# A decoder trunk on eight cores: sums of squares on VectorE, a list scheduler for the order, weights loaded once per tile

**The chip, the cores and the metric.** One Trainium2 chip, all eight cores, two dies of four cores (0 to 3 and 4 to 7). The metric is the device time of the slowest core in microseconds. Executions come in a fast state and a slow one: in the slow state the cores of one die (or of both) show a lower granted TensorE clock and the time is longer. Below, fast runs are compared with fast runs; where a kernel left no fast run, the cores of an undisturbed die are compared, and the text says so.

## The reference, cut to what matters

Four layers on x of (4, 8192, 1024). Even layers mix tokens with a gMLP (spatial gating inside chunks of 128 tokens), odd ones with causal pooling; a SwiGLU of width 2816 follows each. Every sub-layer has an RMS norm in front and one behind.

```python
def rmsnorm(x, g):
    y = xf * lax.rsqrt(jnp.mean(xf * xf, axis=-1, keepdims=True) + EPS)
    ...
def mixer_a(h, ...):
    z = gelu(h @ w_in);  u, v = split(z);  v = layernorm(v)
    sv = einsum('gts,bnsgd->bntgd', tril(w_s), v) + b_s      # 128x128 per group
    return (u * sv) @ w_out
def swiglu(h, ...):
    return (silu(h @ w_gate) * (h @ w_up)) @ w_down
for i in range(4):
    x = x + rmsnorm(mixer(rmsnorm(x, pre)), post)            # A if i even, B if odd
    x = x + rmsnorm(swiglu(rmsnorm(x, pre2)), post2)
```

Each core has half a sequence: 4096 tokens and some earlier ones (the halo) that the mixers look back to.

## The kernel before

Features lie on partitions (8 chunks of 128), tokens on the free axis. A core goes through five tiles of 896 tokens, each split in a half of 512 and one of 384 columns. So that TensorE has work while the norms between two sub-layers run, the output projection goes half by half, and the chain of norms of the first half is meant to lie behind the projection of the second.

An RMS norm needs a sum over partitions. ScalarE squares each of the eight chunks, and a matmul with a matrix of ones adds each square into a PSUM bank, which then holds the sum on every partition:

```python
def stats_mm(fc, first, last):
    pe_mm(PSH(sb_), ONESM[:], SQv(fc), first, last, ...)     # one matmul per square

# PostNorm.chain: steps of a boundary, each with a time worked out by hand
d = (n + 60) / 960.0
a = (n + 240) / 1200.0
r1 = 1.0 + 1.3 + 2 * a + 0.5
for fc in range(1, KC):
    th.append(lambda fc=fc: mult(fc));     times.append(r1 + i * d); i += 1
    th.append(lambda fc=fc: add(fc - 1));  times.append(r1 + i * d); i += 1
    th.append(pre[fc - 1])                 # square + stats_mm of the next norm
    ...
def tick(dt):                              # called after each group of matmuls
    clock["t"] += dt
    while bg and bg[0][0] <= clock["t"]:
        bg.pop(0)[1]()                     # emit the steps that are due by that clock
```

So the program order of every engine is what these estimated times make of it. Weights go through three slots of 1 MB of bf16 (the DMA casts them from fp32: the page of before has 1321 MB read from HBM, where the weight queue moved 650 MB). The code is written to load output weights once for each half, unless a slot still has them; the profile counts 260 loads for SwiGLU's where one for each tile would be 160, 40 for pooling's instead of 20, and only 50 instead of 40 for mixer A's:

```python
NWSLOT = 3
def run_sublayer(hA, hB, head, mid, tail, make_chain, reuse=False):
    ...
    for p, first, last in natural_order(tail):
        p.load(); p.run(hA, first, last)
    drain_all(); add_chain(make_chain(hA))
    for p, first, last in (reuse_order(tail) if reuse else natural_order(tail)):
        p.load(); p.run(hB, first, last)   # load() does nothing if the slot still has it
    drain_all(); add_chain(make_chain(hB))
```

The spatial gating of mixer A comes in one go after all u projections: for each of 16 chunks of 128 features a few matmuls of 128 columns fill a bank, VectorE adds a bias out of that bank and multiplies by u.

Of the kernel before, what the change touches and what calls it, by code (L numbers as in the profile page):

```python
# [14 lines left out]
NCH = 7  # L15
T = NCH * 128
HALVES = ((0, 512), (512, 384))
NTILES = 5
HALO = 3
NCHUNK = NTILES * NCH  # L20
NTOK = NCHUNK * 128
OWN = 4096
DFF = 2816
NJ = DFF // 128
EPS = 1e-6
WSLOT = 4096
NWSLOT = 3
USE_LNEXP = True

GC_MIXPRE, GC_MIXPOST, GC_FFNPRE, GC_FFNPOST, GC_BSCALE, GC_LNB, GC_N = 0, 32, 64, 96, 128, 144, 176  # L30

class Op:
    __slots__ = ("eng", "fn", "deps", "sig", "sigidx", "dsem", "dval", "pos", "gidx", "clk", "ckey")

    def __init__(self, eng, fn, dsem=None, dval=0):
        self.eng = eng
        self.fn = fn
        self.deps = []
        self.sig = False
        self.sigidx = 0  # L40
        self.dsem = dsem
        self.dval = dval

class Sched:
# [9 lines left out]
    def add(self, eng, fn, reads=(), writes=(), dsem=None):  # L54
# [13 lines left out]
        for k in reads:  # L68
            rec = res.get(k)
            if rec is not None and rec[0] is not None:  # L70
                deps[id(rec[0])] = (rec[0], "RAW")
        for k in writes:
            rec = res.get(k)
            if rec is not None:
                if rec[0] is not None and id(rec[0]) not in deps:
                    deps[id(rec[0])] = (rec[0], "WAW")
                for r in rec[1]:
                    if id(r) not in deps:
                        deps[id(r)] = (r, "WAR")
        cand = []  # L80
        for d, kind in deps.values():
            if d is op:
                continue
            if d.dsem is None and op.dsem is None and d.eng == eng:
                if eng == "pe":
                    continue
            cand.append(d)
# [10 lines left out]
        if op.dsem is None:  # L98
            clk[op.ckey] = op.pos
        else:  # L100
            clk[op.ckey] = op.pos
# [71 lines left out]
def build_nc(layers=(0, 1, 2, 3), ntiles=NTILES):  # L173
    nc = bass.Bass("TRN2", target_bir_lowering=False)
    S = Sched()
# [6 lines left out]
    a_w_in = dram("a_w_in", [2, D, 4096])  # L182
    a_w_out = dram("a_w_out", [2, 2048, D])
    b_w_in = dram("b_w_in", [2, D, D])
    b_w_grp = dram("b_w_grp", [2, 4, 256, 256])
    b_w_out = dram("b_w_out", [2, D, D])
    w_gate = dram("ffn_w_gate", [4, D, DFF])
    w_up = dram("ffn_w_up", [4, D, DFF])
    w_down = dram("ffn_w_down", [4, DFF, D])
    gvec_d = dram("gvec", [128, GC_N])  # L190
    lng_d = dram("a_ln_g", [2, 2048])
# [3 lines left out]
    pm_d = dram("poolm", [3, 128, 512])  # L195

    sb = nc.alloc_sbuf_tensor
    X = sb("X", [128, KC * T], F32)
    H = sb("H", [128, KC * T], BF16)
    MS = sb("MS", [128, KC * T], F32)  # L200
    SQ = sb("SQ", [128, KC * T], BF16)
    BIG = sb("BIG", [128, 28672], BF16)
    WR = sb("WR", [128, NWSLOT * WSLOT], BF16)
    RS = [sb("RS0", [128, T], F32)]
    SG = [sb("SG0", [128, T], BF16)]
    GV = sb("GV", [128, GC_N], F32)
    GBC = sb("GBC", [128, 2 * 2048], BF16)
    WSM = sb("WSM", [128, 2 * 1024], BF16)
    BIAS = sb("BIAS", [128, 2 * 2048], F32)
    PM = sb("PM", [128, 3 * 512], BF16)  # L210
    PH = sb("PH", [128, 2 * 1024], BF16)
    ONESM = sb("ONESM", [128, 128], BF16)
    ONES1 = sb("ONES1", [128, 128], BF16)
    EPSC = sb("EPSC", [128, 1], F32)
    ST = sb("STATS", [128, 64], F32)
    ps = nc.alloc_psum_tensor("ps", [128, 4096], F32)

    engsem = {e: nc.alloc_semaphore("sem_" + e) for e in ("pe", "act", "dve")}
    wsem = [nc.alloc_semaphore("sem_w%d" % i) for i in range(NWSLOT)]
    xsem = nc.alloc_semaphore("sem_x")  # L220
    ysem = nc.alloc_semaphore("sem_y")
    _cs = [0]

    def csem_new():
        _cs[0] += 1
        return nc.alloc_semaphore("sem_c%d" % _cs[0])

    class Half:
        def __init__(self, h, col, n):
            self.h, self.col, self.n = h, col, n  # L230
            self.c_lo, self.c_hi = col // 128, (col + n) // 128

    cur = {"hc": None}

    def rng():
        hc = cur["hc"]
        return hc.col, hc.n

    def on(hc, fn):
        def run():  # L240
            old = cur["hc"]
            cur["hc"] = hc
            try:
                fn()
            finally:
                cur["hc"] = old
        return run

    def fm(buf, fc):
        c, n = rng()  # L250
        return buf[:, fc * T + c: fc * T + c + n]

    def Xv(fc): return fm(X, fc)
    def Hv(fc): return fm(H, fc)
    def MSv(fc): return fm(MS, fc)
    def SQv(fc): return fm(SQ, fc)
    def kX(fc): return ("X", fc, cur["hc"].h)
    def kH(fc): return ("H", fc, cur["hc"].h)
    def kMS(fc): return ("MS", fc, cur["hc"].h)

    def blocks(name, lo, n):
        return tuple((name, b) for b in range(lo // 128, (lo + n + 127) // 128))

    def kSQ(fc):
        c, n = rng()
        return blocks("SQ", fc * T + c, n)

    def bigfm(off, fc):
        c, n = rng()
        return BIG[:, off + fc * T + c: off + fc * T + c + n], blocks("BIG", off + fc * T + c, n)  # L270

    VOFF = 16 * T
    PLOFF = 7 * 1024
    MXOFF = PLOFF + 8 * T
    def Uv(fc): return bigfm(0, fc)[0]
    def kU(fc): return bigfm(0, fc)[1]
    def Gv(j): return bigfm(0, j)[0]
    def kG(j): return bigfm(0, j)[1]
    def PLv(fc): return bigfm(PLOFF, fc)[0]
    def kPL(fc): return bigfm(PLOFF, fc)[1]  # L280
    def MXv(fc): return bigfm(MXOFF, fc)[0]
    def kMX(fc): return bigfm(MXOFF, fc)[1]
    def Vv(c, c0=0, n=2048): return BIG[:, VOFF + c * 2048 + c0: VOFF + c * 2048 + c0 + n]
    def kV(c, c0=0, n=2048): return blocks("BIG", VOFF + c * 2048 + c0, n)
    def PTv(c, c0=0, n=1024): return BIG[:, c * 1024 + c0: c * 1024 + c0 + n]
    def kPT(c, c0=0, n=1024): return blocks("BIG", c * 1024 + c0, n)

    def RSv():
        c, n = rng()
        return RS[0][:, c:c + n]  # L290
    def kRS(): return ("RS", cur["hc"].h)
    def SGv():
        c, n = rng()
        return SG[0][:, c:c + n]
    def kSG(): return ("SG", cur["hc"].h)

    def PSH(bank, c0=0, n=None):
        if n is None:
            n = rng()[1]
        return ps[:, bank * 512 + c0: bank * 512 + c0 + n]  # L300
    def kPSb(bank): return (("ps", bank),)
    def STATb(): return 6 + cur["hc"].h

    state = {"bank": 0, "w": 0, "use": 0}
    slot_use = [0] * NWSLOT

    def next_bank():
        b = state["bank"]
        state["bank"] = (b + 1) % 6
        return b  # L310

    def pe_mm(out, lhsT, rhs, start, stop, reads, writes):
        S.add("pe", lambda e: e.matmul(out, lhsT=lhsT, rhs=rhs, start=start, stop=stop), reads, writes)  # L313

    def act(out, in_, func, reads, writes, scale=None, bias=None, accum=None):
        kw = {}
        if scale is not None:
            kw["scale"] = scale
# [239 lines left out]
    def drain_all():  # L558
        while bg:
            bg.pop(0)[1]()  # L560
# [443 lines left out]
```

## Time and profile before

| | |
|---|---|
| median of four runs | 7614.7 us (7203.2 to 8100.2) |
| profiled run, fast | 7201.6 us, every core 7174 to 7202 |
| matmul columns (counted in the built program) | 14,243,840 = 5935 us at 2.4 GHz |
| TensorE busy | 6353.6 us |
| all waits of TensorE that the trace names | 829 us |

The 2.4 GHz, and the 2.5 ns that are counted below for each matmul, can be read from dense rows of this trace: 44 matmuls of 512 columns take 9.66 us (from 3126.17 us) and 32 of 384 take 5.36 us (from 3700.62 us). Less the 0.16 us by which the record of a single matmul reaches into the next, these are 216 and 162.5 ns each. The 128 columns between them take 53.4 ns, 2.4 columns in a ns, and some 2.5 ns are left for each matmul.

The page's line of the weight queue (packets, MB, share of the time of 16 engines):

```profile
q0 software_dynamic: 1118784, 650.31, 69.4%
```

A stretch of one spatial gating as a window, where the columns are length, busy time and count of TensorE, of its weight loads, of VectorE, ScalarE and GpSimd, the granted clock, the DMA share and GB/s:

```profile
2877.00:2900.00 23.00, 11.49 (x98) 7.01 (x95) 21.99 (x41) 0.87 (x2) 1.14 (x1) 0.67 0.36 47
```

VectorE is full (21.99 of 23 us) and TensorE half empty: it does four matmuls in 0.38 us and mostly stops for 0.8 to 1.3 us until VectorE has emptied a bank.

### The profile page before, as it was taken

To read this page: it belongs to the slowest core of one execution; us is meant where nothing else is said; L and a number is where in the kernel's file an instruction comes from. 1 tells how busy PE (TensorE), PEld (TensorE's weight loads), DVE (VectorE), ACT (ScalarE), POOL (GpSimd) and SP (SyncE) were. 2 spreads that over 40 slices of the span, in tenths; PEclk is the share of its full clock that TensorE was granted. 3 is DMA by queue.
4 is the path that set the end of the run, shared out by engine and by line. 5 is a ranking of instruction groups with operands and counts; after the bars stand their busy time and mean duration, and the time that the engine had idled before them with its cause. 6 is when DMAs were issued, how large, how long until landed. Compare 5 with 4: busy or idle time off the path is not lost.

```text
span 7201.6 us, 92363 instructions; the slowest of 8 cores (7174.3 to 7201.6 us)
## 1 busy us (share of the span) xinstructions
PE 6353.6 (88%) x34464; PEld 3276.1 (45%) x34464; DVE 2101.7 (29%) x3733; ACT 2473.5 (34%) x4765; POOL 878.9 (12%) x936
## 2 busy tenths in 40 slices
PE   6978887898989998899989988999899889898988
PEld 3545554444444444444444434444444444444444
DVE  4222321322243222422142214231423242324231
ACT  3242422434242424233423333243424242424241
POOL 0111111011101110111111100111011101110111
PEclk9999998899999999999999999999999999999999
DMA  6698699668665877586757674777487756875687
GB/s 106 88 118 111 91 129 124 98 78 111 90 85 77 108 92 122 66 107 88 97 68 103 92 130 64 100 99 93 60 101 103 123 76 79 112 96 70 86 108 102
DMA packets 1143119, 693.60 MB, mean 96 GB/s; under 512 B 17568, under 2 KB 1132832, under 8 KB 1142560
## 3 DMA queue, kind: packets, MB, share of 16 engines
q0 software_dynamic: 1118784, 650.31, 69.4%
q1 hardware_dynamic: 23904, 37.39, 1.5%
q8 instruction: 290, 4.75, 0.3%
q14 instruction: 141, 1.16, 0.1%
HBM read 1321.10 MB, written 16.78 MB: 186 GB/s over the span
## 4 chain that ended last, share of the span: by engine, by line
PE 68%; DMA 12%; ACT 8%; issue 6%; DVE 6%; SPq 0%; ACTq 0%; DVEq 0%; POOL 0%; POOLq 0%
PE ps L313 68%; DMA WR<-ffn_w_down 4%; ACT SQ L323 4%; DMA WR<-a_w_in 3%; DMA WR<-b_w_in 2%; DVE MS L446 2%; DVE MS L743 2%; DMA WR<-ffn_w_up 1%; ACT L323 1%; DMA X<-xT 1%; ACT RS L323 1%; DVE X L451 1%; ACT BIG L323 1%; DVE BIG L730 1%; ACT SG L323 1%
## 5 line engine op out<-in xcount | busy, mean ns | idle before, releaser
L313 PE MATMUL ps<-H,WR 128*128 128x384 bf16 (+2 forms) x16640 | 3042.2, 344 | 42.8 <-DMA WR<-ffn_w_up 19.5
L313 PE MATMUL ps<-BIG,WR 128*128 128x384 bf16 (+3 forms) x11200 | 2162.4, 348 | 116.9 <-DMA WR<-ffn_w_down 97.1
L313 PEld LDWEIGHTS ps<-H,WR 128*128 128x128 bf16 x16640 | 1616.0, 98 | 1414.3 <-issue 83.5
L313 PEld LDWEIGHTS ps<-BIG,WR 128*128 128x128 bf16 x11200 | 1092.0, 99 | 1069.3 <-issue 204.9
L605 DVE TENSOR_TENSOR BIG<-ps,SG 128x384 bf16<-128x384 f32 (+3 forms) x880 | 526.0, 598 | 2141.4 <-ACT SG L323 2139.8
L323 ACT ACTIVATE SG<-ps 128x384 bf16<-128x384 f32 (+3 forms) x880 | 459.5, 522 | 1878.6 <-PE ps L313 1850.4
L323 ACT ACTIVATE SQ<-ps 128x384 bf16<-128x384 f32 (+3 forms) x640 | 334.7, 523 | 1798.8 <-PE ps L313 1798.8
L446 DVE TENSOR_TENSOR MS<-MS,RS 128x384 f32<-128x384 f32 (+3 forms) x640 | 371.9, 591 | 1780.4 <-ACT RS L323 1780.4
L313 PE MATMUL ps<-SQ,ONESM 128*128 128x384 bf16 (+3 forms) x1280 | 452.4, 354 | 451.6 <-ACT SQ L323 450.6
L313 PE MATMUL ps<-WR,H 128*128 128x512 bf16 x3216 | 759.9, 388 | 62.9 <-DMA WR<-a_w_in 41.0
L323 ACT ACTIVATE BIG<-ps 128x512 bf16<-128x512 f32 (+3 forms) x882 | 455.6, 563 | 497.5 <-PE ps L313 478.4
L407 DVE SCALAR_TENSOR_TENSOR H<-X,GV,RS 128x384 bf16<-128x384 f32 (+2 forms) x640 | 374.8, 656 | 531.4 <-ACT RS L323 531.4
L313 PEld LDWEIGHTS ps<-WR,H 128*128 128x128 bf16 x3216 | 317.0, 99 | 442.0 <-issue 104.0
L338 POOL DMA_DIRECT2D WR<-ffn_w_down x260 | 277.9, 1069 | 1716.8 <-PE ps L313 1716.4
L313 PEld LDWEIGHTS ps<-SQ,ONESM 128*128 128x128 bf16 x1280 | 125.9, 98 | 761.0 <-issue 708.6
L338 POOL DMA_DIRECT2D WR<-ffn_w_gate x220 | 192.3, 874 | 2148.4 <-PE ps L313 2148.4
L323 ACT ACTIVATE SQ<-X 128x384 bf16<-128x384 f32 (+2 forms) x640 | 335.2, 558 | 260.1 <-DVE X L451 180.7
L323 ACT ACTIVATE MS<-ps,GV 128x384 f32<-128x384 f32 (+3 forms) x640 | 394.0, 616 | 0.0
L451 DVE TENSOR_TENSOR X<-MS,X 128x384 f32<-128x384 f32 (+3 forms) x560 | 327.7, 592 | 0.0
L323 ACT ACT_TABLE_LOAD x161 | 206.6, 1283 | 149.3 <-PE ps L313 70.6
L313 PE MATMUL ps<-SQ,BIG 128*128 128x128 bf16 x1072 | 136.4, 272 | 133.3 <-DVE MS L743 129.7
L338 POOL DMA_DIRECT2D WR<-ffn_w_up x220 | 194.1, 882 | 0.2 <-issue 0.2
(45 smaller groups left out, 1579.2 us busy)
## 6 DMA issues: line engine op xcount, KB each, us to landing
WR<-ffn_w_down POOLq DMA_DIRECT2D x260, 704.0 KB, 9.0
WR<-ffn_w_gate POOLq DMA_DIRECT2D x220, 512.0 KB, 7.1
WR<-ffn_w_up POOLq DMA_DIRECT2D x220, 512.0 KB, 9.1
WR<-a_w_in POOLq DMA_DIRECT2D x80, 1024.0 KB, 11.6
WR<-a_w_out POOLq DMA_DIRECT2D x50, 1024.0 KB, 9.3
WR<-b_w_in POOLq DMA_DIRECT2D x40, 1024.0 KB, 10.6
WR<-b_w_out POOLq DMA_DIRECT2D x40, 1024.0 KB, 9.4
X<-xT SPq DMA_DIRECT2D x40, 256.0 KB, 8.7
```

Of the source, the lines that this page charges most:

```text
L313: S.add("pe", lambda e: e.matmul(out, lhsT=lhsT, rhs=rhs, start=start, stop=stop), reads, writes)
L323: S.add("act", lambda e: e.activation(out=out, in_=in_, func=func, **kw), reads, writes)
L338: S.add("pool", lambda e, dst=dst, src=src: e.dma_start(out=dst, in_=src), (), wk, dsem=wsem[w])
L407: dve(lambda e: e.scalar_tensor_tensor(out=o, in0=a, scalar=g, in1=rr, op0=ALU.mult, op1=ALU.mult), (kX(fc), ("GV",), kRS()), (kH(fc),))
L446: dve(lambda e: e.tensor_tensor(out=o, in0=o, in1=rr, op=ALU.mult), (kMS(fc), kRS()), (kMS(fc),))
L451: dve(lambda e: e.tensor_tensor(out=x, in0=m, in1=x, op=ALU.add), (kMS(fc), kX(fc)), (kX(fc),))
L605: dve(lambda e, o=o, a=a, sgv=sgv: e.tensor_tensor(out=o, in0=a, in1=sgv, op=ALU.mult), kPSb(bu_) + (kSG(),), kG(j))
L730: dve(lambda e: e.tensor_tensor(out=u, in0=m, in1=u, op=ALU.mult), (kMS(ptmp),) + kU(pfc), kU(pfc))
L743: dve(lambda e, o=o, a=a, bb=bb: e.tensor_tensor(out=o, in0=a, in1=bb, op=ALU.add), kPSb(b) + (("BIAS", j),), (kMS(tmp),))
```

## The change

The intent: fewer columns on TensorE and fewer stops. It is nearly a new program; the parts that the argument touches are these (cuts marked with dots, the rest of 1767 lines of diff left out).

```diff
-    def stats_mm(fc, first, last):
-        pe_mm(PSH(sb_), ONESM[:], SQv(fc), first, last, ...)
+    class Stats:
+        def add(self, src, ksrc, psum):
+            t_act(..., o, src, AF.Square, ...)                       # square into one of 3 buffers
+            if i == 0:
+                t_dve(... tensor_copy(out=acc, in_=o()))             # fp32 accumulator
+            elif i < KC - 1:
+                t_dve(... tensor_tensor(out=acc, in0=acc, in1=o(), op=ALU.add))
+            else:
+                t_dve(... tensor_tensor(out=fin, in0=acc, in1=o(), op=ALU.add))   # bf16, "SQF"
+        def rstd(self):
+            t_pe((-1,) + self.prio, [(bank, ONESM[:], fin, True, True, ...)])     # ONE matmul per norm
+            t_act(... AF.Ln); t_act(... AF.Exp, scale=-0.5)
```
```diff
-    def tick(dt): ...                      # order by hand
+    class Graph:
+        def place(self, pools):
+            # list scheduling over all instructions of the program: each task has an engine, a duration,
+            # a priority and predecessors; the engine that is free first takes its best ready task;
+            # PSUM banks, weight slots and square buffers are handed out at placing time
+            ...
+def d_act(n, psum=True): return ((61 if psum else 112) + n) / 1200.0
+def d_dve(n, rate=1):    return (66 + n / rate) / 960.0
+order = G.place({"ps": range(1, 8), "pss": range(1), "W": range(NSLOT), "SQ": range(3), "SG": range(3)})
```
```diff
-NWSLOT = 3
+NSLOT = 6
+            tp = [Piece(wf_dn[l, q]) for q in range(6)]     # loaded once, both halves use it
+            for h in range(2):
+                out_proj(s, vout[h], tp, NJ, ...)
-        spp = [Piece(None, sp_work(...)) for q in range(4)] # gating after all u projections
+            for ub in range(4):
+                for h in range(2): a_u(s, vout[h], ub, pcs[4 + ub])
+                for h in range(2): a_spatial(s, vout[h], ub, j)   # priority (0, s, 0, 4 + ub, 2, ...)
-HALO = 3                                                    # chunks of 128
+HALO = 256
+        return (((0, 512), (112, 512)), ((112, 512), (128, 512)), ((128, 512), (240, 512)),
+                ((240, 512), (256, 512)))[l]                # first tile: columns that each layer still needs
```

Besides, the group matmul of the pooling mixer is folded into its output weights once on the chip, the pooling looks back with 16 columns instead of 128, the weights are repacked by the host into pieces of 1 MB with rows of 512 B in SBUF, and the normalisation of v becomes one bf16 instruction.

## The prediction

> **What bounds the kernel now.** I read the page first, then the spans and clocks of all cores, the waits of TensorE, the timeline of one sub-layer boundary, and stretches of 180 us with their clocks.
>
> ```profile
> span 7201.6 us, 92363 instructions; the slowest of 8 cores (7174.3 to 7201.6 us)
> PE 6353.6 (88%) x34464; PEld 3276.1 (45%) x34464; DVE 2101.7 (29%) x3733; ACT 2473.5 (34%) x4765; POOL 878.9 (12%) x936
> PEclk9999998899999999999999999999999999999999
> ```
>
> TensorE is the bound; no other engine is above 34%. All cores lie within 0.4% of each other at a mean clock of 0.96, so this execution is a fast one. The four timed runs were 7203, 7500, 7730 and 8100 us: only one was like the profile.
>
> I counted the moving columns of all matmuls in both built programs. Before: 14,243,840, which at 2.4 GHz are 5935 us. Hence 7201.6 - 5935 = 1267 us are not streaming. The waits of TensorE say where most of them are:
>
> ```profile
> PE ps L313 <- ACT SQ L323: 450.6, 577, 12.9
> PE ps L313 <- DVE MS L743: 141.8, 207, 1.3
> PE ps L313 <- DMA WR<-ffn_w_down: 97.1, 72, 4.6
> PE ps L313 <- DMA WR<-a_w_in: 41.0, 18, 5.3
> PE ps L313 <- DMA WR<-ffn_w_up: 19.5, 16, 4.3
> PE ps L313 <- DMA WR<-b_w_in: 18.1, 14, 2.5
> ```
>
> The columns after the names are total us, times, longest. The largest is the wait for the squares of the RMS norms: each of the 1280 squared tiles is summed over partitions by a matmul with a matrix of ones, and TensorE, which works in order, stops until ScalarE has made the square. The second is the spatial gating, where matmuls of 128 columns come faster than VectorE empties their banks. The four DMA rows are 176 us. The group of the statistics itself:
>
> ```profile
> L313 PE MATMUL ps<-SQ,ONESM 128*128 128x384 bf16 (+3 forms) x1280 | 452.4, 354 | 451.6 <-ACT SQ L323 450.6
> L313 PE MATMUL ps<-SQ,BIG 128*128 128x128 bf16 x1072 | 136.4, 272 | 133.3 <-DVE MS L743 129.7
> ```
>
> Their columns (542,720) need only 226 us, the busy record is 452 because an isolated matmul shows its pipeline, and another 451 us is idle in front. The timeline shows one such stop, and the dense rate beside it:
>
> ```profile
> 3125.95 0.38 PE L313 MATMUL ps<-SQ,ONESM 128*128 128x512 bf16 x1 [0.90 <-ACT SQ L323]
> 3126.17 9.66 PE L313 MATMUL ps<-BIG,WR 128*128 128x512 bf16 x44
> ...
> 3287.18 0.32 PE L313 MATMUL ps<-SQ,ONESM 128*128 128x384 bf16 x1 [2.62 <-ACT SQ L323]
> 3287.34 1.84 PE L313 MATMUL ps<-H,WR 128*128 128x512 bf16 x4
> ```
>
> [...]the start of the 44-matmul row to its end less the 0.16 us pipeline tail is 9.5 us, 216 ns each. [...]after the 2.62 us gap, four matmuls took 1.84 us where they take 1.02 elsewhere, and stretches with sub-layer boundaries granted 0.91 while dense ones granted 0.99 to 1.00. So a removed gap pays twice. [...]the trace has 685 for MS<-MS,RS, and consecutive ones start about 0.60 us apart. [...]the trace has 161 loads of 1283 ns.
>
> **The change, part by part.** It is nearly a new kernel with the same plan (five tiles of up to 896 tokens in two halves).
>
> 1. Statistics: VectorE adds the eight squares into an fp32 accumulator and one matmul per norm sums over partitions. Matmuls go from 1280 to 160 and from 226 to 28 us of columns: -198. The 451 us of waits fall to 160 possible ones.
> 2. Halo of 256 tokens instead of 384, and the first tile trimmed to columns instead of chunks: gate/up and u projections (ps<-H,WR) go from 2935.5 to 2890.7: -45.
> 3. The group matmul of the pooling mixer is folded into its output weights once, on the chip (64 matmuls, +14). With the smaller halo, ps<-BIG,WR goes from 1973.8 to 1889.9: -84. The pooling matmul on the preceding chunk streams 16 columns instead of 128: -24.
> 4. Together 13,433,856 columns in 33,076 matmuls: 5597 us at 2.4 GHz, 337 less than before.
> 5. Weights: repacked on the host into 1 MB pieces (2048 rows of 512 B on the SBUF side), six slots instead of three, each piece loaded once per tile and used by both halves. 484 such loads are 508 MB against 650 MB on that queue. Before, 1,118,784 packets took 69.4% of 16 x 7201.6 us, or 71 ns each; a piece is then 2048 x 71 / 16 = 9.1 us. A full SwiGLU takes 17 pieces = 155 us against 197 us of columns, mixer A 12 = 110 against 149. Loads fit under the matmuls.
> 6. Spatial gating stands between the u matmuls, so TensorE has other work while VectorE empties banks: most of the 142 us go. Normalising v becomes a bf16 tensor_scalar instead of a 2345 ns scalar_tensor_tensor.
> 7. Order: instead of ticks written by hand, a list scheduler places all instructions. In the built order one sum matmul per norm stands between long runs of matmuls, and the first half of the next sub-layer starts with its k steps spread, as the normalised tiles come.
>
> Costs: 1120 accumulating adds (343 of 512 at 685 ns, 700 of 384 at 551, the rest smaller, 653 us) and 160 copies (about 70) on VectorE. Its normalisation of v shrinks by about 150 us, so VectorE ends near 2650 us, 44% of 6000. The functions in the built order change table set 249 times instead of 161: +88 x 1.28 = 113 us on ScalarE, which ends near 2500. Neither bounds the middle; both lie in the chain at a boundary.
>
> That chain, for a half of 512 (estimate): Ln and Exp 0.7 + 0.6, with a load 1.3; eight of multiply, add and accumulate at 0.60 pitch = 14.4; sum matmul 0.4; Ln, Exp 1.3; first normalised tile 0.75: about 20 us. Behind it lies the other half's output projection: 29 us in SwiGLU, 20.5 in mixer A, about 22 in mixer B. So it is nearly covered: I give 3 us for each of 40 boundaries.
>
> Sum for a fast run: columns 5597; 2.5 ns x 33,076 = 83; start 50 (first dense matmul came at 59 us before; the x loads now stand before most of the setup) and final chain and store 20; boundaries 40 x 3 = 120; DMA waits 60 of 176; gating and pooling waits 40; lost clock 50. That is 6020 us, or 0.836 of the profiled run.[...]
>
> **The rivals.** (a) The accumulation takes the place of the wait removed: 24 VectorE operations stand where 16 stood, and TensorE waits in order for the sum matmul. For it: mixer A's cover equals the chain, and VectorE also serves the other half there. Against: the order was placed with a delay for every step. It would cost 6 to 8 us a boundary instead of 3: 6150 to 6220. (b) Weight loads become the bound: the same bytes per column in less time, all rows now 512 B. For it: stretches of the first tile had a DMA share of 0.95 to 1.00 with the clock at 0.82 to 0.94. Against: the sum of 5. It would give about 6200. (c) The denser TensorE is throttled: columns fill 93% of the time instead of 82%. For it: three of four timed runs were slow already. Against: the profile grants 0.99 to 1.00 in stretches of 180 us that are 97% busy on all cores. It would give 6400 to 7050.
>
> **Range and chances.** Fast runs should lie at 5900 to 6250. A median over runs of both states can lie higher, as the 7615 before against 7203. I put the figure a little above the fast estimate, at 6120, with 5900 to 6700. [...]fast against fast the gain is some 16%, so faster 0.97, within 2% 0.02, slower 0.01.
>
> **What would show it.** TensorE's wait for squares should be gone and the wait for the last accumulator (SQF) be under 150 us in all; ps<-SQF,ONESM x160 under 60 us busy; TensorE busy about 5850 at a clock of 0.98; VectorE near 2650; table loads 249; software queue 508 MB. Wrong would be: SQF waits over 300 us (rival a), DMA waits on WR over 200 us (rival b), or a clock under 0.95 in stretches without gaps (rival c).

## The result

| | before | after |
|---|---|---|
| median of all runs | 7467.5 us (16 runs, 7194.9 to 8202.1) | 6585.7 us (10 runs, 6078.8 to 7192.0) |
| fast runs | 7195 to 7248 us | 6079 to 6133 us |
| ratio of fast runs | | 0.846, 95% interval 0.842 to 0.850 |
| profiled run | 7201.6 us, clock 0.96 | 6077.3 us, clock 0.980 to 0.981 |

A ratio is the mean time of one kernel's fast runs over that of the other's fast runs of the same rounds, so it is not quite the ratio of the medians. The kernel is faster by 15.4% in the fast state. The median of 6586 us is a mixture: in six of the ten runs one die was slow. In the slowest, die 1 took 7174 to 7190 us at a clock of 0.804 to 0.806 while die 0 took 6070 to 6077 us at 0.98, in the same execution.

The page of the kernel after:

```profile
span 6077.3 us, 92409 instructions; the slowest of 8 cores (6070.0 to 6077.3 us)
PE 5790.4 (95%) x33076; PEld 3133.8 (52%) x33076; DVE 2703.9 (44%) x4972; ACT 2497.6 (41%) x5127; POOL 554.2 (9%) x489
...
q0 software_dynamic: 999120, 507.82, 71.6%
```

TensorE is busy 95% of the time instead of 88%, with 563 us less of busy time. Its waits:

```profile
PE ps L476 <- DVE SQF L543: 116.0, 47, 14.5
PE ps L476 <- DVE H L568: 69.2, 29, 4.6
PE ps L476 <- ACT BIG L458: 34.6, 10, 10.4
PE ps L476 <- DVE MS L754: 15.7, 37, 1.4
PE ps L476 <- DMA WR<-wa_in: 11.5, 2, 7.2
```

The squares are gone from the list, SQF (the accumulated sum) and H (the normalised tiles behind it) stand in their place with 185 us, the gating (MS) fell from 142 to 16 us, and the DMA rows from 180 to 13 (a row of 1.4 us for gate and up weights is not shown). In all, the named waits fell from 829 to 264 us. The group of the sum matmuls (busy us, mean ns, then the idle time before them):

```profile
L476 PE MATMUL ps<-SQF,ONESM 128*128 128x384 bf16 (+4 forms) x160 | 55.3, 346 | 116.8 <-DVE SQF L543 116.0
```

Where are the stops that are left? The longest of them lie where a tile ends and the next one begins, because the last output projection is the end of the tile and the next tile's x has still to be normalised. TensorE in one such change:

```profile
3704.31 0.59 PE L476 MATMUL ps<-SQF,ONESM 128*128 128x512 bf16 x1 [13.41 <-DVE SQF L543]
3707.51 16.09 PE L476 MATMUL ps<-WR,H 128*128 128x512 bf16 x64 [2.62 <-DVE H L568]
```

With one of 1.84 us before and one of 3.08 us after these, the stops of this change add up to 21 us; the four tile changes have 18 to 22 us each, 82 us together. Another 13.5 us of the SQF row is the first norm of the run, before any projection. The stop of 13.4 us seen on the other engines, a few lines of the same stretch:

```profile
3695.83 0.68 DVE L540 TENSOR_TENSOR ACC<-ACC,SQ 128x512 f32<-128x512 f32 x1
...
3696.94 0.63 ACT L458 ACTIVATE SQ<-X 128x512 bf16<-128x512 f32 x1 [1.72 <-DVE ACC L540]
...
3698.43 0.68 DVE L540 TENSOR_TENSOR ACC<-ACC,SQ 128x512 f32<-128x512 f32 x1
```

Successive adds of the 512-column half stand 2.1 to 2.6 us apart, because VectorE has the multiplies and adds of the other half (384 columns) between them, and ScalarE's next square waits until an add has given one of the three square buffers free.

An account of the 1124 us between the two profiled runs. The granted clock enters as columns / clock - columns, a rough estimate, since the clock on the page is a mean over the whole span:

| | before | after | difference |
|---|---|---|---|
| columns at 2.4 GHz | 5935 | 5597 | 338 |
| columns at the granted clock, in excess of that (0.96, 0.98) | 247 | 114 | 133 |
| waits of TensorE by name | 829 | 264 | 565 |
| 2.5 ns for each matmul | 86 | 83 | 3 |
| not assigned | 105 | 19 | 86 |
| span | 7202 | 6077 | 1124 |

So the columns are a third of the gain. The rest is stops, and the clock that goes with them, but for 86 us that no row explains. The clock record in the two traces, of which the pages show means, has only two values on all eight cores, full and half (1.00 and 0.50): core 6, the slowest in both, was at half clock for 561 us before and for 244 us after. The question for the experiments is which part of the change removed them.

### The profile page after: what moved, and what is told of

Read it like the earlier page. It is cut to its first block, busy times and chain, and to the rows that moved or that the text cites. A ratio compares the mean times of both kernels' runs of the same rounds, so it can differ in the third digit from the quotient of the medians.

```text
span 6077.3 us, 92409 instructions; the slowest of 8 cores (6070.0 to 6077.3 us)
## 1 busy us (share of the span) xinstructions
PE 5790.4 (95%) x33076; PEld 3133.8 (52%) x33076; DVE 2703.9 (44%) x4972; ACT 2497.6 (41%) x5127; POOL 554.2 (9%) x489
## 4 chain that ended last, share of the span: by engine, by line
PE 82%; DVE 8%; issue 5%; ACT 3%; DMA 1%; DVEq 0%; ACTq 0%; SPq 0%; POOL 0%; POOLq 0%
PE ps L476 82%; DVE ACC L540 2%; DVE MS L592 2%; DVE H L568 2%; ACT RS L458 1%; ACT SQ L458 1%; DMA WR<-wa_in 1%; ACT BIG L458 1%; DMA w_s<-BIG 1%; ACT L458 1%; DVE SQF L543 1%; DVE MS L754 1%; DVE X L598 0%; DVEq L314 0%; DVE BIG L724 0%
## 5 line engine op out<-in xcount | busy, mean ns | idle before, releaser
L476 PE MATMUL ps<-BIG,WR 128*128 128x384 bf16 (+4 forms) x10880 | 1959.1, 340 | 10.2 <-DVE MS L754 3.9
L653 DVE TENSOR_TENSOR BIG<-ps,SG 128x384 bf16<-128x384 f32 (+4 forms) x880 | 515.7, 590 | 1538.7 <-PE ps L476 1428.4
L458 ACT ACTIVATE SG<-ps 128x384 bf16<-128x384 f32 (+4 forms) x880 | 448.7, 517 | 1603.9 <-PE ps L476 1600.7
L540 DVE TENSOR_TENSOR ACC<-ACC,SQ 128x384 f32<-128x384 f32 (+4 forms) x960 | 566.8, 593 | 746.7 <-ACT SQ L458 671.3
L458 ACT ACTIVATE MS<-ps 128x384 f32<-128x384 f32 (+4 forms) x640 | 332.4, 519 | 1020.9 <-PE ps L476 1017.8
L592 DVE TENSOR_TENSOR MS<-MS,RS 128x384 f32<-128x384 f32 (+4 forms) x640 | 368.3, 586 | 213.3 <-ACT RS L458 213.3
L458 ACT ACTIVATE SQ<-X 128x384 bf16<-128x384 f32 (+3 forms) x640 | 341.6, 557 | 228.9 <-DVE X L598 75.2
L568 DVE SCALAR_TENSOR_TENSOR H<-X,GV,RS 128x384 bf16<-128x384 f32 (+3 forms) x640 | 371.1, 649 | 100.5 <-ACT RS L458 100.3
L458 ACT ACT_TABLE_LOAD x249 | 319.5, 1283 | 149.8 <-PE ps L476 126.1
L598 DVE SCALAR_TENSOR_TENSOR X<-MS,GV,X 128x384 f32<-128x384 f32 (+4 forms) x560 | 356.2, 646 | 0.0
L458 ACT ACTIVATE SQ<-ps 128x384 bf16<-128x384 f32 (+4 forms) x640 | 329.7, 520 | 25.2 <-DVE ACC L540 19.2
## 6 DMA issues: line engine op xcount, KB each, us to landing
WR<-wa_in POOLq DMA_DIRECT2D x80, 1024.0 KB, 16.7
WR<-wa_out POOLq DMA_DIRECT2D x40, 1024.0 KB, 12.4
```

The lines of the kernel that those rows point to most:

```text
L458: return e.activation(out=out() if callable(out) else out, in_=in_() if callable(in_) else in_, func=func, **kw)
L476: return e.matmul(out(), lhsT=lhsT() if callable(lhsT) else lhsT, rhs=rhs() if callable(rhs) else rhs, start=start, stop=stop)
L540: t_dve(self.prio + (1,), lambda e: e.tensor_tensor(out=acc, in0=acc, in1=o(), op=ALU.add), [kq, ka], [ka], v.n)
L568: t_dve(CH + (s, v.h, 1), lambda e, o=o, a=a, g=g, r=r: e.scalar_tensor_tensor(out=o, in0=a, scalar=g, in1=r, op0=ALU.mult, op1=ALU.mult), ...
L592: t_dve(CH + (s, v.h, 0), lambda e: e.tensor_tensor(out=m, in0=m, in1=r, op=ALU.mult), kf("MS", v, fc) + [("RS", v.h)], kf("MS", v, fc), v.n)
L598: t_dve(CH + (s, v.h, 0), lambda e: e.scalar_tensor_tensor(out=o, in0=m, scalar=g, in1=x, op0=ALU.mult, op1=ALU.add), kf("MS", v, fc) + kf ...
```

## The experiments

The eleven runs below were spread over three chips; the kernel before ran in fast state at 7201 to 7216 us on each of them (7267 once), so that differences of 1% or more between chips can be read. The kernel after was not run again beside them. All results were correct. A slow die shows in the clock record of the kept traces too, as stretches at 0.81: in the profiled run of experiment 6 there are 1989 to 2081 us of them on the cores of die 0 and none on cores 4 and 5. Column counts are of the built programs.

### 1. The kernel before, with the sums on VectorE

Step 1 of the prediction alone, the order left to the hand-written ticks. The accumulators needed room, so the gating bias became bf16.

```diff
     def stats_mm(fc, first, last):
-        pe_mm(PSH(sb_), ONESM[:], SQv(fc), first, last, ...)
+        if first:
+            dve(... tensor_copy(out=acc, in_=sq))
+        elif not last:
+            dve(... tensor_tensor(out=acc, in0=acc, in1=sq, op=ALU.add))
+        else:
+            dve(... tensor_tensor(out=fin, in0=acc, in1=sq, op=ALU.add))
+            pe_mm(PSH(sb_), ONESM[:], fin, True, True, ...)
```

> The kernel before with its hand-made order, but the eight squares of a norm are added on VectorE and one matmul per norm sums over partitions (1280 sum matmuls become 160; the bias table is held in bf16 to make room). My theory, that the stops at the squares are removed by having one sum matmul per norm: 198 us of columns and most of the 451 us of waits go, fast run near 6650 us, TensorE's wait for the squares' sum under 150 us. Rival, that only the scheduler's order removed those stops: the hand order asks for the sum before VectorE has it, the waits come back under the accumulator's name (300 us or more), fast run 6950 to 7200 us.

Measured: 8275, 8444, 8490 and 8531 us beside 7213 us. Probably no die was undisturbed in any of them (the clocks were 0.80 to 0.90), so the size is uncertain. The least disturbed die took 7867 to 7907 us at a clock of 0.895 to 0.898. Its clock can't be set beside that of a disturbed die of the kernel before, because half clock counts in it as well: in the profiled run core 5 was at half clock for 1575 us (561 before) and at 0.81 for another 2860 us. Its mean clock of 0.84 leaves some 536 us as the loss in the latter, beside half of 1575; without them its 8274 us would be about 7740 us, an estimate. So it is slower than before by some 540 to 700 us, with 198 us less of columns. The rival had the waits right in kind (300 us or more under the accumulator's name), and both theories missed the time. The first wait of TensorE:

```profile
PE ps L315 <- DVE SQF L394: 1179.4, 144, 47.2
```

The sums are 160, and 144 of them stopped TensorE, for 1179 us against the 451 us of waits for squares before. In the longest of these stops the sum matmul waits 47.23 us (to 3022.80 us), and 26 matmuls of the projection under way start only behind it, without a wait of their own. VectorE in this stop:

```profile
2971.97 0.43 DVE L390 CAST ACC<-SQ 128x512 f32<-128x512 bf16 x1 [8.31 <-ACT SQ L325]
2972.32 0.68 DVE L458 TENSOR_TENSOR MS<-MS,RS 128x512 f32<-128x512 f32 x1
...
2980.66 0.69 DVE L392 TENSOR_TENSOR ACC<-ACC,SQ 128x512 f32<-128x512 f32 x1 [7.06 <-ACT SQ L325]
```

In this order each accumulation stands right behind its square and in front of the next chunk's multiply. VectorE stands still until ScalarE has made the square, 8.31 and 7.06 us in these lines (at this tile change ScalarE itself waits 9.58 and 8.06 us for the DMA to bring the chunk that it squares), and the multiply of the next chunk starts only behind the accumulation, 0.35 us after it in the first case: a round trip for each of the eight chunks in place of a pipeline. The lines show the extreme, with a load of x in the loop; at an ordinary boundary of this run (1999 to 2007 us) the adds of 384 columns stand about 2.2 us apart, and the sum matmul behind them stops TensorE for 12.5 us. With a matmul as the adder it was TensorE that waited for a square (450.6 us), and VectorE went ahead.

### 2. The kernel after, with one sum matmul per square

The opposite: only step 1 undone, everything else left to the scheduler, which makes a new order for it. The two halves sum in two banks of their own.

```diff
-            if i == 0: t_dve(... tensor_copy ...)
-            elif i < KC - 1: t_dve(... add ...)
-            else: t_dve(... add to SQF ...)
+            t_pe((-1,) + self.prio, [(bank, ONESM[:], o, i == 0, i == KC - 1, ...)])
...
-    order = G.place({"ps": range(1, 8), "pss": range(1), ...})
+    order = G.place({"ps": range(1, 7), "pss0": (0,), "pss1": (7,), ...})
```

> The changed kernel with one sum matmul per square again (1280 instead of 160, +195 us of columns and 3 us of issue), placed by the same scheduler; two banks kept for sums, six for the rest. My theory (stops are made by the many small sums): +198 us of columns and about 250 us of waits and pipeline time, near 6530 us. Rival (the scheduler hides the stops): only the columns come back, 6250 to 6300 us, with waits for squares under 80 us.

Measured: 6229 and 6231 us, ratio to before 0.864 (0.861 to 0.866); 150 us slower than after, close under the rival's range. It has 195 us more of columns (223 in place of 28).

```profile
PE ps L476 <- ACT SQ L458: 51.7, 56, 3.9
...
PE ps L476 <- DVE H L559: 29.4, 11, 4.7
```

Here 1280 sum matmuls wait for squares, and they wait 52 us in all, not 451. So fewer places to wait, to which the prediction put it down, were not needed for the wait to fall. What this program has in place of the old one is above all the order, which experiments 3 and 4 vary alone; the new slots, halo and gating are in it too. The sums on VectorE bring less than their columns, because the chain through VectorE costs 104 us more of stops (SQF and H 185 us in after, SQ and H 81 here). Not all of the 150 us need be the sums: two banks for them leave six for the rest in place of seven, and the waits for the gating (MS) are 64 us here against 16 in after.

### 3. The same instructions in another order

The scheduler is told that ScalarE and VectorE take half their time; it then places their consumers too early. Matmuls and VectorE instructions are the same in number; only ScalarE's table loads, which follow from the order, go from 249 to 221.

```diff
-    return ((61 if psum else 112) + n) / 1200.0        # d_act
+    return 0.5 * ((61 if psum else 112) + n) / 1200.0
-    return (66 + n / rate) / 960.0                     # d_dve
+    return 0.5 * (66 + n / rate) / 960.0
```

> The changed kernel, same instructions, but the scheduler is told that VectorE and ScalarE take half as long, so it places sum matmuls and the next sub-layer's first matmuls about 8 to 10 us too early at each of 80 boundaries. If the order is what keeps the boundary chain covered: waits for the last accumulator and the normalised tiles rise from 185 us to 500 or more, 6400 to 6700 us. If the engines' slack covers it whatever the order: under 6180 us.

Measured: 6648 us in the fast run (every core 6616 to 6646, clock 0.944 to 0.949), 568 us slower than after, as the theory had it (some 550 us on cores 2 to 7, since cores 0 and 1 had about 135 us at 0.81). Core 0:

```profile
PE ps L476 <- DVE SQF L543: 501.6, 129, 14.9
```

129 of the 160 sum matmuls stop TensorE in place of 47. The named waits rise by some 420 us, and the clock falls from 0.98 to about 0.947, which for 5597 us of columns is another 200 us by the estimate above (half clock for 699 us in place of 244). The two together are somewhat more than was measured, so the split is rough.

### 4. Matmul sums in that order

Experiments 2 and 3 together, to see whether matmul sums suffer as much from a bad order.

```diff
+ the edits of experiments 2 and 3
```

> Both changes of the two earlier runs at once: one sum matmul per square (1280), and the scheduler told that VectorE and ScalarE take half as long. If the stops at the squares in the kernel before came from their place in TensorE's order and not from their number: waits for squares come back to 300 us or more (52 us with the true durations), run near 6600 to 6800 us. If their number alone were harmless and their place too: under 6350 us.

Measured: each of the four runs had one slow die; the undisturbed dies took 6481 to 6503 us at a clock of 0.98. A core of the undisturbed die waits:

```profile
PE ps L476 <- ACT SQ L458: 151.6, 278, 6.8
```

The time is 274 us over experiment 2, less than expected: the wait for squares came back only in part. All six combinations in one table (slowest core; fast runs, undisturbed dies for the two marked):

| order | sums on VectorE | sum matmuls |
|---|---|---|
| the scheduler's | 6079 | 6229 |
| the scheduler's with halved durations | 6648 | 6503 (undisturbed die) |
| the hand order of before | 8275 (7907 on the least disturbed die) | 7201 |

Along a row the sums differ (and, in the first two rows, the bank that they take), and the sign turns: moving them to VectorE saves 150 us in the good order, costs 145 us in the blind one, and more in the hand order (some 540 to 700 us by the estimate at experiment 1). Of these three orders, it pays only in the one that keeps the chain through VectorE covered.

### 5. The first tile untrimmed

The plainest term of the prediction: is a column worth its time at 2.4 GHz? All layers of tile 0 work on all 512 columns of the first half.

```diff
-        return (((0, 512), (112, 512)), ((112, 512), (128, 512)), ((128, 512), (240, 512)), ((240, 512), (256, 512)))[l]
+        return (((0, 512), (0, 512)), ((0, 512), (0, 512)), ((0, 512), (0, 512)), ((0, 512), (256, 512)))[l]
```

> The changed kernel without the trimming of dead columns in the first tile (kept for the last output only): 381,440 more columns, 159 us at 2.4 GHz, all in the first tile; the result stays right. If TensorE's columns set the time there: +159 us, near 6240 us. Rival, that weight loads or the chains set the first tile's time (the clock there is 0.90 to 0.92 in stretches, with a DMA share near 1): under +80 us.

Measured: 6227 us fast (undisturbed dies 6215 to 6226), 148 us slower than after, for 381,440 columns or 159 us. The waits stayed (SQF 117.6 us, H 66.7). TensorE's columns set the time nearly one to one in this kernel.

### 6. The spatial gating after all u projections

Step 6 undone: only the priority of the gating is changed.

```diff
-            t_pe((0, s, 0, 4 + ub, 2, v.h, q), mms, alloc=b)
+            t_pe((0, s, 0, 8, 2, v.h, fc), mms, alloc=b)
```

> The changed kernel with the spatial gating of mixer A placed after all its u matmuls, as before, instead of between them; everything else equal. If the interleaving removed the 142 us of waits for emptied banks: they come back by 80 to 130 us (10 mixers), near 6180 us. Rival, that seven banks and the scheduler hide it anyway (half 1 u matmuls, output projection of half 0): within 20 us of 6079 us.

Measured: 6293 us fast (undisturbed dies 6282 to 6294, clock 0.961), 214 us slower than after, more than either theory. The wait is what the profile of before had, on a core of the undisturbed die:

```profile
PE ps L476 <- DVE MS L754: 147.0, 167, 1.5
```

That is 131 us more than in after. The rest goes with the clock, which by the estimate above costs some 110 us more here (half clock for 493 us on this core). The same kind of stretch, a gating, in this run:

```profile
3938.00:3969.00 31.00, 14.53 (x118) 8.51 (x116) 29.85 (x52) 0.49 (x1) 1.14 (x1) 0.61 0.27 35
```

and in the kernel after, where u projections stand between:

```profile
3775.00:3820.00 45.00, 43.62 (x308) 25.16 (x306) 31.35 (x54) 17.52 (x31) 4.56 (x4) 1.00 0.60 71
```

With VectorE full and TensorE half busy the clock is 0.61 on the mean (1.00 until 3944 us, 0.50 from 3946 us on), as it was 0.67 before; with the same VectorE work spread over 45 us in place of 31 it is 1.00. No stop here is longer than 1.5 us. The wait list shows only part of what such a stretch costs.

### 7. Output weights loaded once for each half

Step 5 undone in part: the six slots stay, but the output weights of mixer A and of SwiGLU are loaded anew for the second half (644 loads in place of 484). This goes further than the kernel before, which loaded mixer A's nearly once for a tile: the queue then moves 676 MB, against 650 before and 508 in after.

```diff
-            tp = [Piece(wf_dn[l, q]) for q in range(6)]
             for h in range(2):
+                tp = [Piece(wf_dn[l, q]) for q in range(6)]      # and wa_out in the same way
                 out_proj(s, vout[h], tp, NJ, ...)
```

> The changed kernel, but the pieces of the output projections of mixer A and SwiGLU are loaded again for the second half: 160 more loads of 1 MB (484 to 644), the software queue from 71.6% to about 95% of the 16 engines' time. If loads are hidden with little room left: DMA waits of TensorE rise from 13 us to 100 to 300 us, 6180 to 6400 us. If there is room even so: under 6110 us. If the queue becomes the bound: over 6400 us.

Measured: 6414, 6435 and 6473 us; 335 us slower at least, and the clock of the profiled run 0.956 to 0.963. In each of these runs some cores had lost a little to a disturbance; the undisturbed dies took 6364 to 6381 us, some 300 us more than those of after. The queue and the waits of the profiled run:

```profile
q0 software_dynamic: 1329360, 675.60, 87.9%
```
```profile
PE ps L476 <- DVE SQF L543: 289.7, 79, 15.9
...
PE ps L476 <- DMA WR<-wf_dn: 26.4, 9, 8.2
```

By name the DMA costs this row, 6 us of wa_in and 4 of wb_in, far less than the 100 to 300 us expected, so none of the three expectations describes this run. The large row is SQF, though the chain has not changed. A boundary shows why; TensorE here:

```profile
1958.09 0.48 PE L476 MATMUL ps<-SQF,ONESM 128*128 128x384 bf16 x1 [4.52 <-DVE SQF L543]
```

and at a boundary of the kernel after:

```profile
1791.86 3.62 PE L476 MATMUL ps<-WR,H 128*128 128x512 bf16 x16
1795.86 0.32 PE L476 MATMUL ps<-SQF,ONESM 128*128 128x384 bf16 x1 [0.38 <-DVE SQF L543]
```

There, matmuls of the next sub-layer (WR,H) stand between the last projection and the second half's sum. Here the row before the sum is still the projection (28 matmuls BIG,WR until 1953.57) and then TensorE stands idle. The likely reason is that in the scheduler's model the weights of the next sub-layer get no slot until the reloaded ones are through; the run shows that a wa_in piece lands 26.3 us after its issue in place of 16.7 (medians). Here a load that comes late takes away the cover of a wait, and the wait is put down to the engine that is waited for (SQF 289.7 us, wf_dn 26.4). How much of the 335 us is bandwidth and how much this order, the run does not separate.

### 8. The next tile's x loaded early

The stop of 13.4 us at a tile change is a chain that starts with the load of x. Here the first half of the next tile's x is loaded during the last SwiGLU into a free part of a buffer, and the next mixer's weights no longer wait for it.

```diff
+        if s % 8 == 7 and t + 1 < NTILES:
+            for fc in range(KC):
+                t_dma("sp", (1, s, 0, fc), d, xT3[:, fc, g0:g0 + w0], [], kd, ...)   # d: free tail of BIG
-            gx = [("X", 0, 7)] if s % 8 == 0 and s > 0 else []
+            gx = []
...
+ squares and normalisation of that half read the early copy
```

> The changed kernel, with x of the next tile's first half loaded during the last SwiGLU of a tile into the unused end of the BIG buffers, so that its first norm need not wait for the final add and a load of some 11 us. The trace of the changed kernel shows stops of 13.4 and 2.6 us there at each of four tile changes. If that load is on the path: the stops of over 10 us vanish, 60 to 90 us less with the clock, 5990 to 6020 us. If the final chain on VectorE holds it anyway: under 20 us gained.

Measured: 6138, 6139, 6161 and 6182 us in the fast runs, the best die 6096 to 6110: 20 to 60 us slower than after, so the expectation of a gain failed.

```profile
PE ps L476 <- DVE SQF L543: 72.3, 43, 14.7
PE ps L476 <- DMA WR<-wa_in: 44.1, 12, 7.8
```

SQF fell by 44 us, as meant, and no stop at a tile change is longer than 8.6 us. In its place came waits for the first weights (wa_in, from 11.5 to 44 us), for H (from 69 to 75) and for the gating (from 19 to 41, the rows MS and BIG of VectorE). The stop moved; experiment 10 follows it further.

### 9. A shorter chain through VectorE

The accumulator becomes bf16, so that an add takes 0.43 us in place of 0.69, and ScalarE writes the first square straight into it, so that the 160 copies go. The scheduler is told of the shorter adds, so it makes a new order.

```diff
-    ACC = [sb("ACC%d" % h, [128, HW[h]], F32) for h in range(2)]
+    ACC = [sb("ACC%d" % h, [128, HW[h]], BF16) for h in range(2)]
...
+            if i == 0:
+                t_act(self.prio + (0,), ACC[v.h][:, v.c0:v.c1], src, AF.Square, ...)
+                return
```

> The changed kernel with a shorter chain on VectorE: the accumulator of the squares in bf16 ([...]about 0.33 us instead of 0.60 between starts for 512) and the first square written straight into it by ScalarE, so 160 copies fall away. 8 x 0.27 = 2 us less in each of 80 sums, VectorE some 400 us less busy. If the chain on VectorE makes the remaining 185 us of waits for the last accumulator and the normalised tiles: they fall to 90 to 120 us and the fast run to 5990 to 6030 us. If ScalarE's squares and table loads hold the chain as well: waits above 150 us, 6050 us or more.

Measured: 6006.5 us in the undisturbed fast run and 6072 in one with a partly disturbed die; the undisturbed dies of five of the six runs took 5998 to 6008 us at 0.984, in one run up to 6030, against 6069 to 6080 for those of after. The ratio to before is 0.838, with a wide interval (0.828 to 0.849) from only two fast runs. It beats both kernels, after by 72 us or 1.2% (across chips, with the kernel before at 7201 to 7206 us beside it). A core of an undisturbed die:

```profile
PE ps L476 <- DVE SQF L544: 101.4, 45, 12.9
PE ps L476 <- DVE H L569: 43.2, 19, 4.6
```

The two rows fell from 185 to 145 us, less than expected although the time lies in the expected range, and the clock rose from 0.981 to 0.984 (half clock for 184 us on this core). The pitch of dependent adds in the kernel after, VectorE alone:

```profile
1944.34 0.69 DVE L540 TENSOR_TENSOR ACC<-ACC,SQ 128x512 f32<-128x512 f32 x1 [0.17 <-DVE ACC L540]
1945.21 0.69 DVE L540 TENSOR_TENSOR ACC<-ACC,SQ 128x512 f32<-128x512 f32 x1 [0.17 <-DVE ACC L540]
```

and in this one:

```profile
1911.43 0.43 DVE L541 TENSOR_TENSOR ACC<-ACC,SQ 128x512 bf16<-128x512 bf16 x1 [0.17 <-DVE ACC L541]
1912.03 0.42 DVE L541 TENSOR_TENSOR ACC<-ACC,SQ 128x512 bf16<-128x512 bf16 x1 [0.17 <-DVE ACC L541]
```

0.87 us became 0.60, where the expectation had 0.33, its author's estimate; bf16 adds of 512 columns that do not depend on each other start 0.34 us apart in experiment 11. The longest stop of a tile change only went from 12.4 to 14.5 us down to 11.4 to 12.4 (the 12.9 us in the row above are the first norm of the run); in after, the adds wait there for their turn between the other half's work and not for one another.

### 10. Both together

Experiment 9 with the early load of experiment 8, and the proper copy of x loaded later, after the second half's last normalised tile.

```diff
+ the edits of experiments 8 and 9
-                if nx is not None:
+                if nx is not None and v.h:
                     load_x(nx[0], v.h, nx[1], fc, s)
+            if s % 8 == 0 and s > 0:
+                for fc in range(KC):
+                    load_x(geo[0][0], 0, geo[0][1], fc, s, [("H", 1, KC - 1)])
```

> The shorter chain, with the prefetch of the next tile's first half as in the earlier run (which was 60 us slower than the changed kernel, its weight loads late), but the second load of that x into its own place put off until the second half's norm is done, so that it does not compete with the weights. If the weight loads were what took the prefetch's gain: waits for WR under 20 us, 20 to 70 us faster than the shorter chain alone. If the order that the scheduler finds there (gating without cover, the second half's chain) is the cost: no faster than the shorter chain alone.

Measured: 6045 us in the one fast run, undisturbed dies 5994 to 6043; no faster than experiment 9. A tile change of this run:

```profile
2533.21 0.48 PE L476 MATMUL ps<-SQF,ONESM 128*128 128x384 bf16 x1 [5.88 <-DVE SQF L544]
```

The sum of 384 columns is the second half's; 3.44 us of waiting for H follow. The first half no longer stops TensorE, so its matmuls come sooner and end before the second half's chain is through, and the waits for wa_in come to 35 us. The gain at the tile change is spent on the next link.

### 11. Two accumulators

Experiment 9 with even and odd squares in two accumulators, so that neighbouring adds do not depend on each other.

```diff
-            acc = ACC[v.h][:, v.c0:v.c1]
+            accs = (ACC[v.h][:, v.c0:v.c1], ACC2[v.h][:, v.c0:v.c1])
+            acc = accs[i % 2]
...
+            if i == KC - 1:
+                t_dve(... tensor_tensor(out=fin, in0=accs[0], in1=accs[1], op=ALU.add))
```

> The shorter chain (bf16 accumulator), with two accumulators for the even and the odd squares and one add of the two at the end; the number of operations on VectorE rises by 160 small adds less the 160 first adds (equal). In the shorter chain's trace each dependent add starts 0.60 us after the one before (512 columns: 0.43 of its own and 0.17 of waiting for it), in the changed kernel 0.87. If the dependence of the adds makes the rest of the waits: adds start about 0.4 us apart, the waits for the last accumulator fall from 100 to 60 to 80 us and the fast run from 6006 to 5960 to 5990 us. If ScalarE's squares (0.48 us apart at best) or the loads of x at the tile changes hold it: within 15 us of 6006 us.

Measured: 6080 and 6087 us fast, the faster dies 6046 to 6089: 73 us slower than experiment 9, though SQF and H fell to 92 and 36 us and neighbouring adds now start 0.34 us apart at best (1503.58 and 1503.92 us); neither expectation held. The clock was 0.965 to 0.974 in place of 0.984. Windows of 5 us on a core of the faster die:

```profile
1495.00:1500.00 5.00, 5.00 (x32) 3.01 (x31) 5.00 (x9) 4.04 (x8) 1.14 (x1) 1.00 1.36 167
...
1505.00:1510.00 5.00, 5.00 (x28) 2.73 (x26) 2.50 (x7) 2.43 (x6) 0.00 (x0) 0.81 1.10 261
```

TensorE is busy all of both, yet the second window is granted 0.81. In the twelve windows from 1490 to 1550 us the clock goes 1.00, 1.00, 0.86, 0.81, 0.81, 0.95, 1.00, 0.95, 0.81, 0.81, 0.85, 1.00: dips of 10 to 15 us in a dense stretch. They go on along the whole run, on both dies. On this core the clock record has 48 stretches at 0.81, 577 us in all and mostly 15.2 us long, which cost 19% of that, some 108 us; half clock takes 175 us (its mean clock is 0.968). On core 5 of experiment 9 there is no stretch at 0.81 at all, and 184 us of half clock. So stops were removed, and a second way of losing clock took more than they gave back. Why this run is throttled in that way stays open. One rival was not tested: it was measured on a chip of its own, on which neither the kernel after nor that of experiment 9 was run; the kernel before showed no such loss there (7207 to 7216 us at 0.96 in three of its four fast runs), but it is the less dense one.

## Why the prediction was right or wrong

The prediction was right: 6079 us in the fast state against an estimate of 6020, a ratio of 0.846 against 0.836, and a median of 6586 inside the range, near its upper end because most runs had a slow die. That the median fell inside is partly luck: four of the ten runs took more than the 6700 us of the upper end, and the prediction has no working for how many runs are slow. The slow dies took 6540 to 7190 us, the two slowest 7080 to 7190. The steps of the prediction:

- **Step 1, the sums on VectorE.** The columns were right. The reason for the waits was wrong: "The 451 us of waits fall to 160 possible ones". With 1280 possible ones in the scheduler's order they are 52 us (experiment 2), and with 160 in the hand order 1179 (experiment 1). The waits follow the order, and the sums on VectorE give back 104 of their 195 us. They saved 150 us in all; 48 us of waits for the gating, which experiment 2 has more, may belong to its missing bank.
- **Steps 2 to 4, columns.** Right: 5597 us were counted, and the first tile's trims, taken back, cost 148 us for 159 of columns (experiment 5).
- **Step 5, weights.** "Loads fit under the matmuls" is what the trace shows: 13 us of waits, where the sum had 60. But the step saw the value of loading once only in DMA waits (176 to 60). Taken back, and somewhat further than before, it costs 335 us, most of it in rows of VectorE and in the clock (experiment 7).
- **Step 6, gating.** "Most of the 142 us go": 16 are left. What was not counted is the clock in such a stretch; taken back, the step costs 214 us, 131 of them in the wait (experiment 6).
- **Step 7, the order.** The prediction named it last and gave it no number of its own. With the same matmuls and VectorE instructions, one worse order costs 568 us (experiment 3), the most of any part taken back. That is the price of this bad order, not what the scheduler gained over the hand order: the new program was not run in the hand order.
- **The chain at a boundary.** Mis-sized: 120 us were given to 40 boundaries, SQF and H measured 185, of which 82 lie at four tile changes, which the prediction did not treat apart, and 13.5 at the start. It took a pitch of 0.60 us for the accumulating adds; dependent ones start 0.87 us apart, and at a tile change 2.1 to 2.6. Rival (a) was thus partly real; a shorter chain took 40 us off these two rows and, with the clock, 72 us off the time (experiment 9).
- **The rest of the sum.** Gating and pooling waits 53 us against 40 (rows MS, ScalarE's BIG, and 3 us of VectorE's BIG); lost clock 114 against 50 by the account above; start and end 70, of which 32 are seen outside the rows already counted (11 us of WSM, 2 of issue, 19 not assigned). With +65 at the boundaries and -47 for the DMA, +13, +64 and -38 make up the 57 us between 6020 and 6077: the sum was near because errors of either sign met, which is luck. The 50 us for lost clock did not go with the prediction's own clock of 0.98, which by the same estimate costs 114.
- **What would show it.** SQF was to be under 150 us (116), the sum matmuls under 60 (55.3), TensorE near 5850 (5790), VectorE near 2650 (2704), 249 table loads and 508 MB: all held. Two sums in the prediction's costs don't close as written: 2102 + 653 + 70 - 150 is 2675 us for VectorE, and 2474 + 113 is 2587 for ScalarE, not "near 2500" (2498 measured). Rival (b), loads as the bound, fell. Rival (c), throttling of the denser program, fell in fast runs (0.98); experiment 11 shows something like it (0.965 to 0.974). The slow state is no sign of it, since it was no rarer before: 9 of 16 runs, against 6 of 10 after.

The costs of the parts taken back one by one are 150, 148, 214, 335 and 568 us: 1415 us, more than the 1124 gained. They overlap, since each reacts on the order, and two of them go further than the kernel before did (an arbitrary bad order, more reloads). What stays open is how the 451 us of before divide between the number of sums and their place: in experiment 4 the blind order brought the wait back only to 152 us.

## What to carry to other kernels

A wait in TensorE's list belongs to the place of an instruction in the order as much as to the work that it waits for: move the consumer behind other work before making the producer cheaper, and test a change of work and a change of order apart. Work moved to another engine must be placed with that engine's other work in mind (in experiment 1 a multiply stood behind an add that waited 7.06 us for its square); the same move saved 150 us in one order and cost 145 in another. And count short, repeated stops and late loads by undoing them, since the clock and the lost cover do not appear under their names.

## What the traces show of clock, adds and table loads

- The granted clock of before and after is 1.00 or 0.50. In the gating shown above it goes to 0.50 at 2884.64 us: in the 6.64 us from 2878 us up to there TensorE was busy for 3.28 us and stopped for 1.28 us at most.
- In the profiled run of after all eight cores ran for 6070 to 6077 us at a mean of 0.980 to 0.981, with TensorE 95% busy on the slowest, and their clock record has no stretch at 0.81. Such stretches stand on slow dies (1989 to 2081 us of them on die 0 in the profiled run of experiment 6), and in experiment 11 as repeated dips of mostly 15.2 us.
- fp32 tensor_tensor of 512 columns on VectorE start 0.60 us apart when neighbours are independent (before, 3244.59 and 3245.19 us) and 0.87 us when each waits for the one before (after, 1944.34 and 1945.21 us); in bf16 dependent ones start 0.60 us apart (experiment 9).
- A table load on ScalarE takes 1283 ns (161 of them before, 249 after). The logarithm after a load that began at 3664.11 us of the kernel after began at 3665.41, 1.30 us later.
